# Which items of a mixture-of-experts plan are followed by transposes, scatters and slot numbers

## The chip, the cores and the metric

The kernel runs on one core of one Trainium2 chip. The metric is the device time of one execution in microseconds (us). Every instruction of TensorE (PE), VectorE (DVE), ScalarE (ACT), GpSimd (POOL) and the DMA queues is in the profile of one such execution.

## The reference

One layer of a decoder: RMSNorm, a pooling mixer beside latent attention, an output projection, and then a mixture of 32 experts, of which each of the 512 tokens takes 4. The change lies in the mixture of experts alone. Cut to that part:

```python
logits = (ht @ w_router + b_router).astype(jnp.float32)
top_vals, top_idx = lax.top_k(logits, TOP_K)
gates = jax.nn.softmax(top_vals, axis=-1)
...
def expert_block(args):
    xblk, e = args
    gu = xblk @ w_gate_up[e] + b_gate_up[e]
    gate = jnp.minimum(gu[:, :D_EXPERT], SWIGLU_LIMIT)
    up = jnp.clip(gu[:, D_EXPERT:], -SWIGLU_LIMIT, SWIGLU_LIMIT)
    act = gate * jax.nn.sigmoid(SWIGLU_ALPHA * gate) * (up + 1)
    return act @ w_down[e] + b_down[e]
...
y = y.at[row_tok].add(row_gate[:, None] * yb)
```

The model dimension and the experts' dimension are 1024, everything is float32, and the weights of the 32 experts are 384 MiB, which are read once.

## The kernel before

The first 200 us or so of the span compute the layer up to the router (phase A); the rest is the mixture of experts. The 32 experts stand in 32 **positions**, which are named by their number here. `KINDS` makes 12 of them big (2, 4, 6, ... 24) and 20 small. A big position takes up to 128 tokens. Its float32 weights are split into a high part (`mhi`, cast by ACT, L937) and a low part (`mlo`, a subtraction on DVE, of every fourth half on POOL, L938), and every product is three matmuls: high by high, high by low, low by high. A small position takes up to 64 tokens, and its product uses the float32 weights as they are, in 64 columns of the array; two matmuls run side by side on the two halves of the columns.

A position is 12 **items**: gate/up items 0 to 7 and down items 0 to 3, each with one load of 1 MiB. So there are 384 items. A big item is 12 matmuls of 128 columns (the generators `gate_up` and `down` yield once in its middle), a small one 4 matmul instructions, which the trace shows as 8 records (a yield never comes in it). `interleave` puts the items of two lanes into one order, the list `plan`: the lane x (`onx`) holds the big positions and positions 0 and 31, the lane y the other small ones. Loads are issued 14 items ahead, on SP's queue, into a ring.

Beside the items stands work that is small but has to come at some time. It sits in five **queues** of Python generators, and `step()` lets each queue go on by one step:

- `turn x` and `turn y`: `turn(r)` transposes the activation of a position (`m<-ident,au`, four transposes to a step; two steps for a big position, one for a small one). It is queued after the last gate/up item, and `later(..., 3)` spends three steps first. The result is copied out of PSUM by ACT (`ath`, or `ats` at L1036 for a small position) and, for a big one, by DVE also (`atl`). The down items need it: `step(("turn x",))` or `step(("turn y",))` before a down item 0 runs the queue dry.
- `gather`: `gather(r)` transposes the fetched rows of a position (`m<-ident,xr`, two steps of four transposes). For a big position each of the 8 transposes is split in a **chunk** of its own, ACT's `xgh` (L894) and then DVE's `xgl` (L895), both of which read the PSUM bank; a small pair's is one DVE operation for a step (`xgs`). The first gate/up item of the position needs it.
- `arrive`: slot numbers (`m<-aux,oh`) of a position, and then the indirect DMA that fetches its rows (L881, POOL).
- `rest`: the scatters (`combine`): eight steps, each a pair of matmuls `m<-ybh,sc` and `m<-ybl,sc` (for a big position) or `m<-ysh,ss` and `m<-ysl,ss` (for two small ones) and one addition on DVE into `y` (L1148).

All of this work goes through the PSUM pool `m`, which has **two banks** that are taken in turn; the pools `x` (4 banks) and `y` (2) hold the items' products. A matmul into a bank of `m` waits until the one who used that bank two steps ago has been read out. PE runs strictly in the order in which the program is written, from item 12 on (`InOrder`, L118 is the helper's line for every PE instruction). So where `step()` stands, there the transposes and scatters stand on PE. Before the change `step()` is called at the yield in the middle of a big item and at the end of every item of both lanes:

```python
for _ in gate_up(r, k) if what == "gu" else down(r, k):
    step()
...
step()
```

`turn_at` and `fetch_at` say behind which item a gather and a fetch are queued. At a down item 3, `while ("b" if big(r) else "s") in pending: step()` runs the scatters of the position before dry, since their buffers are written anew there.

Of the kernel before, what the change touches and what calls it, by code (L numbers as in the profile page):

```python
# [51 lines left out]
GAPX, GAPY, GAPN, GAPEND = 5, 2, 1, 3  # L52
TURN, SHORT = 0.2, 3.0
NFREE = 12
FILL1 = 2
FT = 3
FN = ((0, 1), (1, 3), (1, 3), (3, 4))
# [68 lines left out]
def block_kernel(ctx: ExitStack, tc: tile.TileContext, xT, x, pos, vecs, w_in, w_pool, w_qb, w_kvb, w_out,  # L126
# [277 lines left out]
    for g, w in enumerate(WINDOWS):  # L404
        cur, step, lo_ = us[g], 1, 1
# [138 lines left out]
    def out_proj(z, c, tt):  # L544

        cs = slice(c * T, (c + 1) * T)
        for k in range(4):
            if ("out", z, c, k) in wraw:
                parts[z, c, k] = split_w(("out", z, c, k))
        po = {}  # L550
        for k in range(4):
            for t in tt:
                if k == 0:
                    po[t] = pt("po", bufs=5 if c and z else 7)
                ts = slice(t * P, (t + 1) * P)
                mm3(PE, po[t], mix["h", z][:, k, ts], mix["l", z][:, k, ts], *parts[z, c, k], k == 0, k == 3)
                yield
        for t in tt:
            V.scalar_tensor_tensor(y[:, t, cs], po[t], grms[z][:, t:t + 1], y[:, t, cs], op0=ALU.mult, op1=ALU.add)
# [193 lines left out]
    for t in range(NT):  # L753
        for _ in out_proj(1, 1, [t]):
            for _ in range(FILL1):
                while todo and next(todo[0], 0) == 0:
# [26 lines left out]
    def bank(tag):  # L783
        return pools["pm"].tile([P, T], F32, tag=tag, bufs={"x": 4, "y": 2, "m": 2}[tag], name=tag)
# [57 lines left out]
    onehot, slots, xg, yb, scat, actT = {}, {}, {}, {}, {}, {}  # L842

    def big(r):
        return r == "o" or KINDS[r] == "B"

    def onx(r):

        return big(r) or r == 0 or r == E - 1
# [103 lines left out]
    def fixed(r):  # L953
        return r != "o" and r < NFIX

    def biases(r, cs):
        for c in cs:
            bs = bias[:, c * T:(c + 1) * T]
            if big(r):
                PE.matmul(banks[r][c], lhsT=m4b[0:96, r:r + 1].to_broadcast([96, P]), rhs=bs, start=True, stop=False)  # L960
            else:
                q = 64 * (c % 2)
                PE.matmul(banks[r][c // 2][q:q + 64, :], lhsT=m4b[0:96, r:r + 1].to_broadcast([96, 64]), rhs=bs,
                          start=not fixed(r), stop=fixed(r))

    def gate_up(r, k):

        first = r == "o"
        if k == 0:
            banks[r] = [bank("x" if onx(r) else "y") for _ in range(4 if big(r) else 2)]  # L970
        if big(r):

            todo = [(hf, c) for hf in range(2) for c in range(2)] if k < KD - 1 else [
                (hf, c) for c in range(2) for hf in range(2)]
            parts = presplit.pop((r, "gu", k))
            for n, (hf, c) in enumerate(todo):
                cs = slice(c * T, (c + 1) * T)
                if k == 0 and not first:
                    biases(r, [2 * hf + c])
                mm3(PE, banks[r][2 * hf + c], xg[r][0][:, k, :], xg[r][1][:, k, :], parts[hf][0][:, cs],  # L980
                    parts[hf][1][:, cs], first and k == 0, k == KD - 1)
                if n == 1:
                    yield
        else:
            w = wslots.pop((r, "gu", k))
            for c in range(4):
                q = 64 * (c % 2)
                if k == 0 and c % 2 == 0 and not fixed(r):
                    biases(r, [c, c + 1])
                PE.matmul(banks[r][c // 2][q:q + 64, :], lhsT=xg[r][:, k, :], rhs=w[:, c * T:(c + 1) * T],  # L990
                          start=(k == 0 and fixed(r)), stop=(k == KD - 1 and not fixed(r)))

                if k == KD - 1 and c % 2 == 1 and fixed(r):
                    biases(r, [c - 1, c])
# [444 lines left out]
    groups = {}  # L1439
# [6 lines left out]
    def arrive(r):  # L1446

        for q in groups[r]:
            select(q)
            yield  # L1450
            slot_info(q)
        fetch(r)
# [28 lines left out]
    def firsts(g):  # L1481
        return plan.index(("gu", g, 0))
# [4 lines left out]
    bigs = [r for r in range(E) if big(r)]  # L1487
# [6 lines left out]
            assert fetch_at[g] > KD, g  # L1494
    queues = {"turn x": [], "turn y": [], "gather": [], "arrive": [], "rest": []}

    def step(drain=None):

        for name, q in queues.items():
            if drain and name not in drain:  # L1500
                continue
            while q:
                if next(q[0], 0) == 0:
                    q.pop(0)
                elif not drain:
                    break
# [21 lines left out]
    for i, (what, r, k) in enumerate(plan):  # L1528

        PE.on = i >= NFREE  # L1530
        while loaded < min(i + (14 if i > 2 else 9), len(loads)):
            load(*loads[loaded])
            loaded += 1
        if big(r):
            n = xorder.index((what, r, k))
            assert n < nsp
        for g, at in fetch_at.items():
            if at == i:
                queues["arrive"].append(arrive(g))
        for g, at in turn_at.items():  # L1540
            if at == i:
                queues["gather"].append(gather(g))
        if (what, r, k) == ("gu", E - 1, 0):
            gf = mo.tile([P, D], F32, tag="xgh", bufs=1, name="gf")
            dma(gf[0:1, :], g_final)
        if k == 0 and what == "gu" and r > 0:
            assert r in xg, (r, i)
        if what == "dn" and k == 0:
            step(("turn x" if onx(r) else "turn y",))
        if what == "dn" and k == KD // 2 - 1:  # L1550

            while ("b" if big(r) else "s") in pending:
                step()
        if (what, r, k) == ("dn", E - 1, 0):
            step(queues)
            down_last(r, gf)
            break
        for _ in gate_up(r, k) if what == "gu" else down(r, k):
            step()

        ahead = n + 3 if big(r) else 2 if (what, r, k) == ("dn", 0, KD // 2 - 2) else 0
        for v in xorder[nsp:ahead]:
            split_item(v[1], v[0], v[2])
        nsp = max(nsp, min(ahead, len(xorder)))
        if what == "gu" and k == KD - 1:
            if r == E - 1:
                spread(gf)
            queues["turn x" if onx(r) else "turn y"].append(later(turn(r, act(r)), 3))
        if what == "dn" and k == KD // 2 - 1 and r < E - 2:
            if big(r):  # L1570
                queues["rest"].append(later(marked("b", combine([r])), 3))
            elif halfdone[0] is None:
                queues["rest"].append(later(marked("s", combine(["s"], r < NFIX)), 3))
        step()
    rt.close()

    PE.on = False
# [95 lines left out]
```

## Time and profile before

| what | value |
|---|---|
| median of three runs | 1267.49 us (1266.92 to 1268.07) |
| the profiled execution, its own time | 1268.17 us |
| its span in the trace | 1266.4 us |
| PE busy | 1213.0 us, 96% of the span |
| DVE, ACT, POOL busy | 865.4, 542.7, 303.7 us |
| DMA: bytes, mean rate | 435.17 MB, 344 GB/s |

The span is the time between the first and the last instruction in the trace; 1.8 us of the execution lie around it. A timeline row of PE gives the start, the duration, the line, the tiles and the count of equal instructions that follow each other. Since the matmuls overlap at their ends, what a group costs is best read as the difference of two starts. A bracket at a row's end is the idle time of the engine before it, and who released it.

### The profile page before, as it was taken

The page shows a single profiled execution, that of the slowest core. Times are in us where ns is not written, and L with a number is a line of the kernel's source. Part 1 is how long each engine was busy: PE and PEld are TensorE (multiplying, and loading weights), DVE is VectorE, ACT ScalarE, POOL GpSimd, SP SyncE. Part 2 cuts the span into 40 slices and gives each one's busy share as a digit, 9 for nine tenths or more (in the row PEclk, how much of TensorE's full clock was granted, in tenths as well). Part 3 has the DMA queues.
Part 4 walks back from the last instruction along what each step waited for, and adds up shares of the span by engine and source line. Part 5 has one row for each costly group of instructions (what it writes and reads, how often), then busy time and mean ns, then how long its engine had stood idle before and what let it go on. Part 6 is the DMA issues. An engine that isn't in the chain of part 4 may idle for free.

```text
span 1266.4 us, 16525 instructions
## 1 busy us (share of the span) xinstructions
PE 1213.0 (96%) x5597; PEld 697.3 (55%) x5597; DVE 865.4 (68%) x1552; ACT 542.7 (43%) x785; POOL 303.7 (24%) x272
## 2 busy tenths in 40 slices
PE   7979999899999998999999999999999999999994
PEld 6856674345655555555555555555645555555332
DVE  6897674657767676676768667776765876767344
ACT  6466650135525443354354435435434454444013
POOL 2355362112212121221123113221312122212001
PEclk9999999899999998999999999999999999999997
DMA  8312428999999998999998999999999999999981
GB/s 313 100 51 88 146 90 313 409 421 415 416 419 411 404 405 322 360 413 416 402 377 348 420 388 399 402 386 393 381 416 358 361 421 403 377 380 399 422 333 69
DMA packets 86849, 435.17 MB, mean 344 GB/s; under 512 B 9223, under 2 KB 9223, under 8 KB 53992
## 3 DMA queue, kind: packets, MB, share of 16 engines
q1 hardware_dynamic: 82818, 420.43, 83.4%
q0 software_dynamic: 3744, 13.24, 2.7%
q8 instruction: 45, 0.74, 0.2%
q10 hardware_dynamic: 198, 0.39, 0.1%
q14 instruction: 44, 0.36, 0.1%
HBM read 429.71 MB, written 4.33 MB: 343 GB/s over the span
## 4 chain that ended last, share of the span: by engine, by line
PE 74%; DVE 7%; DMA 1%; issue 1%; ACT 1%; POOL 0%; DVEq 0%; ACTq 0%; POOLq 0%
PE x L118 33%; PE y L118 29%; PE m L118 11%; DVE mlo L938 3%; DMA bdraw<-in_b_down_dram 1%; DVE au L1007 1%; ACT mhi L937 1%; DVE oh L859 0%; DVE au L1008 0%; DVE ag L1004 0%; DVE au L1006 0%; DVE xgl L895 0%; DVE ss L1096 0%; DVE y L1130 0%; DVE o L1186 0%
## 5 line engine op out<-in xcount | busy, mean ns | idle before, releaser
L937 ACT CAST mhi<-slot 128x1024 fp32r<-128x1024 f32 x288 | 300.6, 1049 | 260.9 <-PE x L118 236.1
L938 DVE TENSOR_TENSOR mlo<-slot,mhi 128x1024 fp32r<-128x1024 f32 x216 | 288.3, 1347 | 66.3 <-ACT mhi L937 65.8
L938 POOL TENSOR_TENSOR mlo<-slot,mhi 128x1024 fp32r<-128x1024 f32 x72 | 177.4, 2464 | 642.5 <-ACT mhi L937 642.4
L118 PE MATMUL y<-slot,xgs 128*64 128x512 f32 x1152 | 276.0, 602 | 0.0
L1148 DVE TENSOR_TENSOR y<-y,m 128x512 f32<-128x512 f32 x168 | 115.0, 684 | 121.8 <-PE m L118 121.4
L118 PE MATMUL x<-mhi,xgh 128*128 128x512 f32 x384 | 164.0, 427 | 0.0
L118 PE MATMUL x<-mlo,xgh 128*128 128x512 f32 x384 | 152.0, 396 | 0.1
L118 PE MATMUL x<-mhi,xgl 128*128 128x512 f32 x384 | 151.4, 394 | 0.0
L118 PEld LDWEIGHTS y<-slot,xgs 128*64 128x64 f32 x1152 | 76.1, 137 | 130.4 <-issue 126.9
L118 PE MATMUL y<-slot,ats 128*64 128x512 f32 x608 | 144.5, 612 | 0.7 <-ACT ats L1036 0.7
L1005 ACT ACTIVATE as<-ag 128x512 f32<-128x512 f32 x44 | 27.8, 632 | 160.7 <-DVE ag L1004 160.7
L118 PEld LDWEIGHTS x<-mhi,xgh 128*128 128x128 f32 x384 | 72.7, 189 | 25.7 <-issue 12.2
L118 PEld LDWEIGHTS x<-mhi,xgl 128*128 128x128 f32 x384 | 72.1, 188 | 17.0
L118 PEld LDWEIGHTS x<-mlo,xgh 128*128 128x128 f32 x384 | 72.4, 189 | 15.9 <-DVE mlo L938 1.1
L118 PEld LDWEIGHTS y<-slot,ats 128*64 128x64 f32 x608 | 39.7, 138 | 74.3 <-issue 70.5
L118 PE MATMUL x<-mhi,ath 128*128 128x512 f32 x192 | 64.2, 416 | 0.0
L118 PE MATMUL x<-mlo,ath 128*128 128x512 f32 x192 | 61.4, 401 | 0.0
L118 PE MATMUL x<-mhi,atl 128*128 128x512 f32 x192 | 60.9, 398 | 0.0
L1098 ACT ACTIVATE ysh<-y,sl 64x512 fp32r<-64x512 f32 x36 | 24.6, 684 | 80.4 <-PE y L118 80.1
L1100 DVE SCALAR_TENSOR_TENSOR ysl<-y,sl,ysh 64x512 fp32r<-64x512 f32 x36 | 27.0, 750 | 42.4 <-ACT ysh L1098 41.9
L881 POOL DMA_INDIRECT xr<-hrow,idx x21 | 28.7, 1367 | 94.5 <-DVE idx L878 48.7
L894 ACT ACTIVATE xgh<-m,gs 128x128 fp32r<-128x128 f32 x96 | 33.4, 366 | 31.9 <-PE m L118 16.7
(401 smaller groups left out, 1737.1 us busy)
## 6 DMA issues: line engine op xcount, KB each, us to landing
slot<-in_w_gate_up_dram SPq DMA_DIRECT2D x256, 1024.0 KB, 10.4
slot<-in_w_down_dram SPq DMA_DIRECT2D x128, 1024.0 KB, 9.9
wraw<-in_w_in_dram SPq DMA_DIRECT2D x16, 256.0 KB, 5.7
wraw<-in_w_out_dram SPq DMA_DIRECT2D x16, 256.0 KB, 2.6
xtraw<-in_xT_dram SPq DMA_DIRECT2D x8, 256.0 KB, 5.9
y<-in_x_dram SPq DMA_DIRECT2D x4, 512.0 KB, 7.3
hrow<-part POOLq DMA_DIRECT2D x8, 256.0 KB, 3.3
out_dram<-o SPq DMA_DIRECT2D x4, 512.0 KB, 2.7
```

Of the source, the lines that this page charges most:

```text
L118: r = f(*args, **kwargs)
L881: G.indirect_dma_start(out=rows[r], out_offset=None, in_=hrow, in_offset=bass.IndirectOffsetOnAxis(ap=idx[:, 0:1], axis=0), bounds_check=T ...
L894: S.activation(hi[:, d, :], v, AF.Copy, scale=g)
L937: S.copy(hi, src)
L938: eng.tensor_tensor(lo, src, hi.bitcast(F32), op=ALU.subtract)
L1005: S.activation(sg, g, AF.Sigmoid, scale=1.702)
L1007: V.scalar_tensor_tensor(u, u, 1.0, g, op0=ALU.add, op1=ALU.mult)
L1098: S.activation(yh[ps_, c], db[ps_, :], AF.Copy, scale=slots[r][ps_, 6:7])
L1100: V.scalar_tensor_tensor(yl[ps_, c], db[ps_, :], slots[r][ps_, 6:7], yh[ps_, c].bitcast(F32), op0=ALU.mult, op1=ALU.subtract)
L1148: V.tensor_tensor(y[:, t, cs], y[:, t, cs], pb, op=ALU.add)
```

## The change

`step` gets a second argument, `only`, with the names of the queues that may go on. Behind the items of the lane y (from the first item of the first big position on) `only` is `("turn x",)`, and `("turn x", "gather")` where the first gate/up item of a big position lies at most `SOON` = 4 items ahead and its gather hasn't been done. So of a small position's item nothing follows but big positions' transposes; scatters, slot numbers, fetches and the transposes of small positions' activations and rows stand behind items of the lane x, in their middle or at their end. A gather that isn't done at its position's first item is run there.

```diff
+SOON = 4
...
-    def step(drain=None):
+    def step(drain=None, only=None):
 
         for name, q in queues.items():
-            if drain and name not in drain:
+            if name not in (drain or only or queues):
                 continue
...
         if k == 0 and what == "gu" and r > 0:
-            assert r in xg, (r, i)
+            while r not in xg:
+                step(only=("gather",))
...
+        beside = None if onx(r) or i < firsts(bigs[0]) else ("turn x",)
+        if beside and any(0 < firsts(g) - i <= SOON and g not in xg for g in groups if big(g)):
+            beside += ("gather",)
         for _ in gate_up(r, k) if what == "gu" else down(r, k):
-            step()
+            step(only=beside)
...
-        step()
+        step(only=beside)
```

The plan of items, the loads and the ring are the same. PE's lines are L118 before and L119 after. Three places on PE show what moves.

**Place 1: gate/up items 4 to 7 of small position 11, between gate/up items 2 and 3 of big position 8.** The matmuls `y<-slot,xgs` are the small items, four to an item, `x<-...` the big ones, and `m<-ybh,sc` and `m<-ybl,sc` a scatter pair. Before:

```order
L118 MATMUL m<-ybh,sc 128x512
L118 MATMUL m<-ybl,sc 128x512
L118 MATMUL y<-slot,xgs 64x512 x4
L118 MATMUL m<-ybh,sc 128x512
L118 MATMUL m<-ybl,sc 128x512
L118 MATMUL y<-slot,xgs 64x512 x4
L118 MATMUL m<-ybh,sc 128x512
L118 MATMUL m<-ybl,sc 128x512
L118 MATMUL y<-slot,xgs 64x512 x4
L118 MATMUL m<-ybh,sc 128x512
L118 MATMUL m<-ybl,sc 128x512
L118 MATMUL y<-slot,xgs 64x512 x4
```

After:

```order
L119 MATMUL y<-slot,xgs 64x512 x16
L119 MATMUL x<-mhi,xgh 128x512
L119 MATMUL x<-mlo,xgh 128x512
L119 MATMUL x<-mhi,xgl 128x512
L119 MATMUL x<-mhi,xgh 128x512
L119 MATMUL x<-mlo,xgh 128x512
L119 MATMUL x<-mhi,xgl 128x512
L119 MATMUL m<-ybh,sc 128x512
L119 MATMUL m<-ybl,sc 128x512
```

The four small items stand together, and the scatter pairs that stood behind each of them come later, in the middles and at the ends of big items.

**Place 2: the gather of big position 4, in the down items of position 2.** `m<-ident,xr` are the gather's two blocks of transposes, `m<-aux,oh` slot numbers. Before:

```order
L118 MATMUL m<-ident,xr 128x128 x4
L118 MATMUL x<-mhi,ath 128x512 x2
L118 MATMUL x<-mlo,ath 128x512 x2
L118 MATMUL x<-mhi,atl 128x512 x2
L118 MATMUL m<-ident,xr 128x128 x4
L118 MATMUL x<-mhi,ath 128x512 x2
L118 MATMUL x<-mlo,ath 128x512 x2
L118 MATMUL x<-mhi,atl 128x512 x2
```

After:

```order
L119 MATMUL m<-ident,xr 128x128 x4
L119 MATMUL x<-mhi,ath 128x512 x2
L119 MATMUL x<-mlo,ath 128x512 x2
L119 MATMUL x<-mhi,atl 128x512 x2
L119 MATMUL m<-ident,xr 128x128 x4
L119 LDWEIGHTS oh
L119 MATMUL m<-aux,oh 128x4
```

The slot numbers, which use the bank of the first block, now stand right behind the second block; before, items of positions 2 and 3 stood there.

**Place 3: the transposes of small position 15, ahead of its down items.** `m<-ident,au` are the transposes, `y<-slot,ats` the down items that use them, and `x<-...` halves of a down item of position 10. Before:

```order
L118 MATMUL m<-ident,au 128x128 x4
L118 MATMUL x<-mhi,ath 128x512 x2
L118 MATMUL x<-mlo,ath 128x512 x2
L118 MATMUL x<-mhi,atl 128x512 x2
L118 MATMUL y<-slot,ats 64x512 x12
```

After:

```order
L119 MATMUL x<-mhi,ath 128x512 x2
L119 MATMUL x<-mlo,ath 128x512 x2
L119 MATMUL x<-mhi,atl 128x512 x2
L119 MATMUL m<-ident,au 128x128 x4
L119 MATMUL y<-slot,ats 64x512 x16
```

The half of a big item that stood between the transposes and the down items is gone from there.

## Rows read from the trace of the kernel before

**Rows 1.** The page: busy time, share, count; one line of the costliest groups.

```profile
PE 1213.0 (96%) x5597; PEld 697.3 (55%) x5597; DVE 865.4 (68%) x1552; ACT 542.7 (43%) x785; POOL 303.7 (24%) x272
...
L938 DVE TENSOR_TENSOR mlo<-slot,mhi 128x1024 fp32r<-128x1024 f32 x216 | 288.3, 1347 | 66.3 <-ACT mhi L937 65.8
L1148 DVE TENSOR_TENSOR y<-y,m 128x512 f32<-128x512 f32 x168 | 115.0, 684 | 121.8 <-PE m L118 121.4
```

**Rows 2.** Windows: us; busy PE, PEld, DVE, ACT, POOL; PEclk, DMA share, GB/s.

```profile
250.00:400.00 150.00, 150.00 (x686) 81.88 (x683) 103.86 (x158) 65.17 (x84) 29.77 (x14) 1.00 1.02 416
400.00:700.00 300.00, 291.55 (x1318) 167.79 (x1316) 214.25 (x323) 134.06 (x171) 69.19 (x31) 0.98 0.96 385
```

**Rows 3.** Timeline of PE: a scatter pair between halves of a big item.

```profile
508.06 0.40 PE L118 MATMUL m<-ybh,sc 128*128 128x512 f32 x1
...
508.53 0.40 PE L118 MATMUL x<-mhi,xgh 128*128 128x512 f32 x1
```

**Rows 4.** Timeline of PE: two small items; a small item and a scatter pair.

```profile
295.73 3.65 PE L118 MATMUL y<-slot,ats 128*64 128x512 f32 x16
299.32 0.25 PE L118 MATMUL m<-aux,oh 128*128 128x4 f16 x4
...
514.20 1.94 PE L118 MATMUL y<-slot,xgs 128*64 128x512 f32 x8
516.07 0.50 PE L118 MATMUL m<-ybh,sc 128*128 128x512 f32 x1
...
516.74 1.94 PE L118 MATMUL y<-slot,xgs 128*64 128x512 f32 x8
```

**Rows 5.** Timeline of PE: blocks of transposes among small items, and in a big one.

```profile
392.40 0.66 PE L118 MATMUL m<-ident,au 128*128 128x128 f32 x4
...
394.85 0.66 PE L118 MATMUL m<-ident,au 128*128 128x128 f32 x4
...
761.81 0.60 PE L118 MATMUL m<-ident,au 128*128 128x128 f32 x4
762.16 0.48 PE L118 MATMUL x<-mhi,xgh 128*128 128x512 f32 x1
```

**Rows 6.** Timeline of PE at the gather of position 8: blocks, next scatter.

```profile
475.56 0.60 PE L118 MATMUL m<-ident,xr 128*128 128x128 f32 x4
...
477.85 0.60 PE L118 MATMUL m<-ident,xr 128*128 128x128 f32 x4
...
482.69 0.79 PE L118 MATMUL m<-ysh,ss 128*128 128x512 f32 x1 [4.24 <-DVE xgl L895]
```

**Rows 7.** Waits of the whole span: us in total, times, longest.

```profile
PE m L118 <- DVE xgl L895: 9.2, 4, 4.2
```

**Rows 8.** Timeline of PE, ACT and DVE at the gather of position 22.

```profile
1019.64 0.66 PE L118 MATMUL m<-ident,xr 128*128 128x128 f32 x4
...
1020.34 0.37 ACT L894 ACTIVATE xgh<-m,gs 128x128 fp32r<-128x128 f32 x1 [1.82 <-PE m L118]
1021.12 0.37 ACT L894 ACTIVATE xgh<-m,gs 128x128 fp32r<-128x128 f32 x1 [0.42 <-DVE xgl L895]
...
1023.19 0.61 DVE L895 SCALAR_TENSOR_TENSOR xgl<-m,gs,xgh 128x128 fp32r<-128x128 f32 x2 [0.53 <-ACT xgh L894]
...
1028.16 0.25 PE L118 MATMUL m<-aux,oh 128*128 128x4 f16 x4
```

**Rows 9.** Windows behind two waits, columns as in the second group.

```profile
482.60:486.00 3.40, 3.31 (x8) 2.64 (x9) 1.07 (x3) 0.18 (x1) 0.00 (x0) 0.50 1.02 424
486.00:490.00 4.00, 4.00 (x14) 3.14 (x13) 2.00 (x3) 1.63 (x2) 0.00 (x0) 0.69 0.66 270
...
645.00:649.00 4.00, 4.00 (x14) 2.16 (x14) 3.08 (x5) 3.71 (x7) 2.04 (x1) 0.57 0.59 211
```

**Rows 10.** Timeline of ACT and PE: a small position's transposes, their copy, their use.

```profile
763.01 0.58 ACT L1036 COPY ats<-m 128x512 f32<-128x512 f32 x1
...
763.73 1.94 PE L118 MATMUL y<-slot,ats 128*64 128x512 f32 x8
```

## The prediction, made before the changed kernel ran

> **What bounds the kernel now.** I read the busy times first, then the windows, then PE's timeline around the transposes and scatters, then the waits. PE is busy for 96% of the span, no other engine for more than 68% [rows 1]. By stage: from 250 to 400 us PE is busy for all of the 150 us, from 400 to 700 for 291.55 of 300 [rows 2]. So the experts' part is bound by PE, and whatever PE's own order costs or saves counts in full. The DMA share stands at 0.96 to 1.02 there [rows 2], so the weights' stream is nearly a bound too; I come back to that as a rival. The time of PE consists of the items themselves, which the change leaves alone, the price of what stands between them, and some waits. The waits that matter are those for a bank of `m` whose last chunk of a gather isn't split yet: 9.2 us in four waits, the longest 4.2 [rows 7].
>
> All sums below are made against the profiled execution, 1268.2 us; the median of the three runs is 0.7 lower.
>
> **A. What is taken out: returns to small items.** PE uses its array whole for big items, scatters and transposes, and in two column halves for small items, and each change between the two shows in the starts. A pair of scatters between halves of a big item takes 508.06 to 508.53, 0.47 us [rows 3]. A small item with a pair behind it takes 514.20 to 516.74, 2.54 us, while two small items in a row take 295.73 to 299.32, 3.59 us, of which 0.09 is the change at the end, as in the next step, so 1.75 for one [rows 4]. So the same pair costs 0.79 behind a small item that is followed by another: 0.32 more. A block of transposes among small items costs 392.40 to 394.85, 2.45, less 1.75, so 0.70; in a big one 0.35 for the block and 0.09 for the first matmul behind it (0.48 instead of 0.39), 0.44 [rows 5]: 0.26 more. Counted in the two orders from the first big position to item 356, work stands between two small items 80 times before and 28 times after. Of the 52 that go, 38 have scatters and 14 have transposes or slot numbers alone (I take the transposes' price for all of these): 38 x 0.32 + 14 x 0.26 = **-15.8 us**. This is the surest term.
>
> The Trainium skill ("TensorEngine Tiling (Array Packing)", Key Properties) says that a change of the tiling mode drains TensorE; it gives no time for it. The trace agrees in kind, with the 0.32 above.
>
> **B. What takes its place: waits behind big gathers.** Place 2 shows it. The scatters, slot numbers and small transposes that used to be spread over items of both lanes now come at every step in the big lane, and a gather is queued in the same lane. So the third user of `m`, which gets the bank of the gather's first block, comes much sooner after it. When is that bank free? Its four chunks each need ACT and then DVE, and DVE has low parts of weights, 1.35 us each, in its queue among them [rows 1]. Only three big gathers before the change had somebody waiting at their first bank: at position 8 the first block starts at 475.56, the next scatter gets through at 482.69 after a wait of 4.24, 7.13 us later [rows 6]; the other two (positions 12 and 20) lie within 0.2 us of that, with waits of 2.0 and 2.7. These three make 8.9 of the 9.2 us [rows 7]. At the other gathers the next user came 8 to 17 us after the first block and nobody waited, as at position 22: 1019.64 to 1028.16 [rows 8].
>
> In the new order the third user comes, if nothing holds it up, 2.3 us after the first block at positions 4, 8 and 10, 2.75 at 24, about 5.1 to 5.6 at 12, 14, 18 and 22; at 6 and 20 a first wait stands ahead of the second block. (The times are counts of halves of big items, 1.4 us each, and of the blocks, from the rows above.) With the bank free at 7.1 us, the waits are 4.8 at 4, 8 and 10, 4.3 at 24, 3.6 at 6, 2.7 at 20, 1.5 at 12 and 18, 2.0 at 14 and 22: 32.0, less the 8.9 of before, **+23.1 us**. The low end: the bank is free when its fourth chunk is out at the earliest that the trace shows, 1023.19 + 0.35 against 1019.64, 3.9 us [rows 8]; then 6.4 us of waits are left, -2.5 net. The high end: at 12, 14, 18 and 22 the new order of DVE has two evictions of a big position and a low part ahead of the first block's last chunk, about 3 us of work, so that the bank is free at about 10; +35. I take 7.1, the value of the only gathers at which somebody waits, as here.
>
> Why a chunk takes so long is in the rows too: even with both engines free the chunks follow each other 0.78 us apart (1020.34, 1021.12), ACT and DVE by turns [rows 8]. The Trainium skill ("PSUM — Partial Sum Buffer", PSUM bank collisions raise a hardware error) says that two engines must not touch one bank in the same partitions at once, readers included, which speaks against bringing bank users together. The alternation in the rows is what that rule would give; by it no bank is free before 4 x 0.78 = 3.1 us, which doesn't change the sum.
>
> **C. The clock behind such waits.** Behind the wait of 4.24 us the granted clock reads 0.50 from 482.6 to 486 and 0.69 to 490; behind that of position 12, 0.57 from 645 to 649 [rows 9]. (1 - 0.50) x 3.4 + (1 - 0.69) x 4 = 2.9 us lost, and (1 - 0.57) x 4 = 1.7; position 20 reads as 1.7 in the same way, so 6.3 for three waits of 2 us or more, 2.1 each. With eight such waits 16.8, less 6.3: **+10.5** (from -3, if one or two waits are left, to +21).
>
> **D. Transposes of small positions.** They stand directly ahead of their down items in several places (place 3), where half a big item used to lie between. The copy by ACT ends 1.78 us after the start of the transposes at 761.81, and with six big matmuls between, the down items at 763.73 had 0.14 us to spare [rows 5, 10]. Without them PE waits 1.3 us (0.9 to 1.7, as ACT is free or casting a high part); with a scatter pair between, 0.65. Position 9: 1.3; positions 5, 19, 21, 28 and 17, with something between: 5 x 0.65. Positions 15, 23 and 25 are behind gathers and counted there. **+4.6** (2.5 to 6).
>
> **E. A flush.** At position 27's last down item five scatter pairs and two blocks of transposes now stand in a row, since fewer steps were left for them. A pair takes PE 0.47 and DVE's addition 0.68 [rows 1, 3], so at least 5 x 0.21 = 1 us, up to 6 where low parts stand in DVE's queue; **+3.5**.
>
> **F. The last 45 us.** Eight returns fewer (-2.6), ten scatter pairs in a row at position 30 (+3), about 1 to 2 us of today's waits gone: **-1** (-3 to +3).
>
> Indirect fetches are queued later as well; the rows they bring are used a few items later, and place 2 shows the gathers themselves at the same place. I put that at nothing; if the cover is gone, it shows as one more wait of some 2 us. The loads of weights are issued at the same items as before.
>
> **The sum:** -15.8 + 23.1 + 10.5 + 4.6 + 3.5 - 1 = +24.9, so 1293.1 for a profiled execution, 1292 for the median.
>
> **The rivals.**
>
> *The banks come free early.* PE that waits leaves ACT and DVE less to do, and the chunks get through as at position 22, 3.9 us after the block. Then B is -2.5, C is -3 and D to F about +2.5: 1268.2 - 15.8 - 2.5 - 3 + 2.5, **1249**. The point from which it decides is a bank free at about 5.3 us: there B is +5, C about +3 and the whole comes to no change. Against it: the three gathers with a waiting user, all at 7. For it: 7 us is three of twelve, and their order on DVE need not be that of the others.
>
> *The weights' stream becomes the bound.* With PE faster by 18 us, the DMA share of 0.96 to 1.02 leaves perhaps 10 us: **1258**. It only cuts the gain of the first rival.
>
> *The work comes behind small items all the same.* The flushes and `turn x` steps could leave most of the returns in place, and the waits too: about **1266**. The order speaks against it: 28 of 80 are left.
>
> *The long waits.* If the four gathers with evictions ahead of their chunks free their bank at 10 us, B is +35 and C +19: **1313**.
>
> **How the numbers follow.** Forecast, waits at 6 to 9 us: 0.56, between 1276 and 1306. A weaker form with some banks free at 5.5 to 6 us, 1270 to 1276: 0.12. No change, with early and late ones in balance or the work where it was: 0.08. Early banks, with or without the stream as the bound: 0.19. Long waits, over 1308: 0.05. The predicted time is the forecast's. For 8 in 10 the range takes in much of the early case: 1254 to 1308; the forecast's own range is 1276 to 1306. About 0.2% is what a measurement of this kernel can tell from no change. Faster 0.19, same 0.08, slower 0.73.
>
> **What would show it.** A: the starts of small items in a row, 1.75 to 1.8 us apart, and 52 groups fewer between them; PE's time between small items at 0.79 and 0.70 as before where it's left. B: the wait of PE in `m` for `xgl`, 9.2 us before, at about 30 in some ten waits, each ending about 7 us after a gather's first block; if it stays under 12, B is wrong. C: stretches at a granted clock of 0.5 to 0.7 behind those waits. D: waits for `ats` of about 1 us ahead of down items of the small positions. E: a row of scatter pairs at position 27 with waits for `y`. The prediction is wrong if banks come free under 5.3 us after the block, or if PE's waits are in other places than behind the gathers, the new order of the fetches above all.

## The result, and the profile after

The changed kernel takes 1311.46 us (median of four runs, 1310.69 to 1311.87), against 1267.78 for the kernel before in the same comparison: a ratio of 1.0346 (95% interval 1.0332 to 1.036), 43.7 us slower. The prediction was slower, 1292, in a range up to 1308. The direction was right and most of the places were; the size was not.

The page of the kernel after, busy times, and two windows (columns as in rows 2):

```profile
span 1310.1 us, 16514 instructions
...
PE 1214.0 (93%) x5597; PEld 710.9 (54%) x5597; DVE 864.7 (66%) x1552; ACT 543.8 (42%) x785; POOL 311.2 (24%) x272
```

```profile
400.00:700.00 300.00, 279.55 (x1259) 165.89 (x1258) 202.11 (x309) 127.53 (x162) 64.41 (x28) 0.97 0.92 366
700.00:1000.00 300.00, 276.94 (x1243) 157.80 (x1243) 202.90 (x299) 127.59 (x164) 65.74 (x30) 0.97 0.93 365
```

PE is busy for the same time as before [rows 1], 1214 us, and the span is 43.7 us longer. So all of the loss shows as idle PE: 20.4 of 300 us from 400 to 700, 8.4 before [rows 2]. The DMA share has fallen from 0.96 to 0.92, and none of PE's waits from the first big item on is for a load of weights, so the weights' stream isn't what holds PE. The waits of the whole span (us in total, times, longest), as in rows 7:

```profile
PE m L119 <- DVE xgl L896: 36.4, 10, 6.6
...
PE y L119 <- ACT ats L1037: 6.7, 8, 1.6
...
PE m L119 <- DVE y L1149: 3.9, 7, 1.5
...
PE m L119 <- ACT ats L1037: 1.8, 3, 1.2
```

The first of them was 9.2 in four [rows 7]. That PE's busy time is unchanged hides two things of opposite sign: fewer returns to small items, and matmuls that take about twice as long at half clock (a scatter's matmul 0.80 us at 744.82 below, 0.40 in rows 3). To part them I took PE's timeline of each run from the first matmul of a big item to the last matmul, and split it in three: the gaps between records; at half clock, half of the busy time there; and the rest, which holds the work at full clock and so the returns. The part ahead of the first big item has the same code in all kernels but took 269 to 276 us in the profiled executions, which isn't explained here; the table leaves it out. (Half clock means stretches whose granted clock is 0.50.)

| kernel | time, us | part with big items | waits for a big gather | waits for `ats` | other idle | half clock | rest |
|---|---|---|---|---|---|---|---|
| before | 1267.8 | 981.0 | 9.2 | 0.7 | 3.5 | 8.0 | 959.6 |
| after | 1311.5 | 1023.7 | 36.4 | 8.6 | 12.3 | 19.5 | 946.9 |
| scatters_only | 1275.8 | 987.9 | 21.2 | 1.1 | 5.8 | 11.5 | 948.3 |
| all_but_scatters | 1319.9 | 1030.9 | 28.7 | 13.9 | 9.2 | 19.2 | 959.9 |
| hold_after | 1294.8 | 1006.7 | 19.7 | 7.8 | 14.1 | 16.4 | 948.6 |
| turn_y_after | 1300.2 | 1010.2 | 35.1 | 1.6 | 10.3 | 17.6 | 945.6 |
| fast_before | 1256.5 | 971.4 | 0 | 2.7 | 4.0 | 4.8 | 959.9 |
| fast_after | 1267.1 | 978.3 | 3.0 | 12.6 | 11.5 | 3.1 | 948.0 |
| four_ops_after | 1268.4 | 980.8 | 4.7 | 11.5 | 11.8 | 4.8 | 948.1 |
| fast_turn_y | 1250.6 | 961.5 | 1.9 | 1.6 | 10.9 | 0 | 946.9 |
| fast_scatters | 1249.2 | 963.3 | 2.4 | 1.1 | 6.7 | 4.8 | 948.2 |
| fast_turns_gathers | 1258.6 | 971.7 | 4.2 | 1.6 | 10.7 | 4.8 | 950.4 |

(The times are medians, the other columns come from one profiled execution each. Most lie within 3 us of the median; that of fast_before took 1263.4, that of all_but_scatters 1324.5.) From before to after: rest -12.7, gather waits +27.2, `ats` +7.9, other idle +8.8, half clock +11.5, and 1.0 ahead of the first big item: +43.7.

### The profile page after: what moved, and what is told of

It reads as the page before. It is cut to its first block, busy times and chain, and to the rows that moved or that the text cites. A ratio compares the mean times of both kernels' runs of the same rounds, so it can differ in the third digit from the quotient of the medians.

```text
span 1310.1 us, 16514 instructions
## 1 busy us (share of the span) xinstructions
PE 1214.0 (93%) x5597; PEld 710.9 (54%) x5597; DVE 864.7 (66%) x1552; ACT 543.8 (42%) x785; POOL 311.2 (24%) x272
## 4 chain that ended last, share of the span: by engine, by line
PE 82%; DVE 11%; ACT 3%; issue 2%; DMA 0%; SPq 0%; DVEq 0%; ACTq 0%
PE x L119 32%; PE y L119 30%; PE m L119 9%; PE po L119 3%; PE acc L119 3%; DVE mlo L939 3%; ACT mhi L938 2%; PE s L119 1%; PE pa L119 1%; DVE xgl L896 1%; DVE y L1149 1%; PE pp L119 1%; PE rows L119 1%; DVE oh L860 0%; ACT ats L1037 0%
## 5 line engine op out<-in xcount | busy, mean ns | idle before, releaser
L939 POOL TENSOR_TENSOR mlo<-slot,mhi 128x1024 fp32r<-128x1024 f32 x72 | 183.0, 2541 | 700.8 <-ACT mhi L938 700.7
L119 PE MATMUL y<-slot,xgs 128*64 128x512 f32 x1152 | 273.6, 609 | 0.0
L119 PE MATMUL x<-mhi,xgh 128*128 128x512 f32 x384 | 164.6, 429 | 0.0
L119 PEld LDWEIGHTS y<-slot,xgs 128*64 128x64 f32 x1152 | 80.4, 139 | 143.1 <-issue 140.5
L119 PE MATMUL x<-mlo,xgh 128*128 128x512 f32 x384 | 151.9, 396 | 1.5 <-DVE mlo L939 1.3
L119 PE MATMUL x<-mhi,xgl 128*128 128x512 f32 x384 | 151.2, 394 | 0.0
L119 PE MATMUL y<-slot,ats 128*64 128x512 f32 x608 | 141.2, 613 | 6.7 <-ACT ats L1037 6.7
L119 PEld LDWEIGHTS x<-mhi,xgh 128*128 128x128 f32 x384 | 72.7, 189 | 34.5 <-issue 21.1
L119 PEld LDWEIGHTS y<-slot,ats 128*64 128x64 f32 x608 | 42.1, 140 | 89.6 <-issue 79.7
L119 PEld LDWEIGHTS x<-mlo,xgh 128*128 128x128 f32 x384 | 72.4, 188 | 17.2 <-DVE mlo L939 2.8
L119 PEld LDWEIGHTS x<-mhi,xgl 128*128 128x128 f32 x384 | 72.1, 188 | 17.2
L119 PE MATMUL x<-mhi,ath 128*128 128x512 f32 x192 | 66.3, 428 | 0.0
L119 PE MATMUL x<-mlo,ath 128*128 128x512 f32 x192 | 62.0, 405 | 0.0
L119 PE MATMUL x<-mhi,atl 128*128 128x512 f32 x192 | 61.5, 403 | 0.0
L119 PEld LDWEIGHTS x<-mhi,ath 128*128 128x128 f32 x192 | 34.3, 196 | 19.0 <-issue 13.8
```

The costliest lines, as they stand in the source:

```text
L119: r = f(*args, **kwargs)
L939: eng.tensor_tensor(lo, src, hi.bitcast(F32), op=ALU.subtract)
```

## The mechanism in one gather

PE's timeline of the kernel after at the gather of position 14, where the trace of before shows no wait:

```profile
734.58 0.60 PE L119 MATMUL m<-ident,xr 128*128 128x128 f32 x4
...
736.42 0.60 PE L119 MATMUL m<-ident,xr 128*128 128x128 f32 x4
...
739.16 0.62 PE L119 MATMUL x<-mhi,atl 128*128 128x512 f32 x2
744.82 0.80 PE L119 MATMUL m<-ysh,ss 128*128 128x512 f32 x1 [5.04 <-DVE xgl L896]
```

and DVE's and ACT's timelines in the same stretch:

```profile
736.15 1.23 DVE L939 TENSOR_TENSOR mlo<-slot,mhi 128x1024 fp32r<-128x1024 f32 x1
737.41 0.35 DVE L896 SCALAR_TENSOR_TENSOR xgl<-m,gs,xgh 128x128 fp32r<-128x128 f32 x1
738.02 0.61 DVE L896 SCALAR_TENSOR_TENSOR xgl<-m,gs,xgh 128x128 fp32r<-128x128 f32 x2 [0.26 <-ACT xgh L895]
739.56 1.72 DVE L939 TENSOR_TENSOR mlo<-slot,mhi 128x1024 fp32r<-128x1024 f32 x1 [0.93 <-ACT mhi L938]
741.20 0.59 DVE L896 SCALAR_TENSOR_TENSOR xgl<-m,gs,xgh 128x128 fp32r<-128x128 f32 x2
741.72 1.39 DVE L1067 SCALAR_TENSOR_TENSOR ybl<-x,sl,ybh 128x512 fp32r<-128x512 f32 x2
743.04 1.21 DVE L939 TENSOR_TENSOR mlo<-slot,mhi 128x1024 fp32r<-128x1024 f32 x1
744.17 0.59 DVE L896 SCALAR_TENSOR_TENSOR xgl<-m,gs,xgh 128x128 fp32r<-128x128 f32 x2
```

```profile
738.48 1.05 ACT L938 CAST mhi<-slot 128x1024 fp32r<-128x1024 f32 x1 [0.23 <-ACT xgh L895]
739.44 0.61 ACT L895 ACTIVATE xgh<-m,gs 128x128 fp32r<-128x128 f32 x2
739.95 1.26 ACT L1066 ACTIVATE ybh<-x,sl 128x512 fp32r<-128x512 f32 x2
```

The scatter that follows gets through at 744.8, when the seventh chunk (the second of the pair at 744.17) is out. It is the seventh and not the fourth because the program's order on DVE alternates between the two banks: in the built program, whose tile numbers the trace leaves out, the chunks of this gather read `m_6256`, `m_6283`, `m_6256`, `m_6283` and so on. The first bank holds out until its fourth chunk, which is the seventh of the eight. Two low parts of weights and two evictions of position 12 lie among them, in DVE's order, which doesn't know that PE waits. Over the whole kernel, the user that waits gets through at the seventh chunk at positions 8, 10, 12, 14, 16, 18 and 22, at the fourth at 4, 6 and 24, where the order on DVE has the first bank's four in a row (at 6 it is the gather's own second block that waits). In the program of the kernel before, of these gathers only 4 and 8 alternate in this way: with PE's order the change has altered DVE's order too. The pool doesn't hand out its banks strictly in turn, as I put it ahead of the prediction. At position 12 a scatter stands between the blocks:

```profile
649.44 0.60 PE L119 MATMUL m<-ident,xr 128*128 128x128 f32 x4
649.79 0.48 PE L119 MATMUL m<-ysh,ss 128*128 128x512 f32 x1
...
652.03 0.66 PE L119 MATMUL m<-ident,xr 128*128 128x128 f32 x4
...
662.10 1.11 PE L119 MATMUL m<-ident,au 128*128 128x128 f32 x4 [6.62 <-DVE xgl L896]
```

The second block starts 2.6 us after the first with hardly a wait, in the scatter's bank, since the first block's is in use for 10 us more.

## The experiments

All edits are to the changed kernel unless the label says before. The order of PE was changed only where the edit says so.

**One operation empties the bank.** fast_after and fast_before:

```diff
             if big(r):
-                for i in range(4):
-                    split_rows(4 * b + i, v[:, i, :])
+                hs, ls = hi[:, 4 * b:4 * b + 4, :], lo[:, 4 * b:4 * b + 4, :]
+                xv = mo.tile([P, 4, P], F32, tag="ag", bufs=1, name="xv")
+                V.tensor_tensor(xv, v, gs[:, 4 * b:4 * b + 4].unsqueeze(2).to_broadcast([P, 4, P]), op=ALU.mult)
+                S.copy(hs, xv)
+                V.tensor_tensor(ls, xv, hs.bitcast(F32), op=ALU.subtract)
```

> The changed kernel, but a big gather's bank is emptied by one DVE operation of four chunks into SBUF (0.7 us), from which ACT and DVE then make the high and low parts; nothing else moves. Theory (the chain of eight ACT-DVE chunks holds the bank, and both the waits and the half clock come from it): PE's waits for the gather's evictions fall from 36 us to under 8, stretches at half clock from 51 us to under 15, time 1311.5 - 29 - 18 = about 1264 (1255 to 1275). Rival (the bank is late because DVE works through low parts of weights first, however few operations the eviction has): waits of 20 us are left, half clock 30 us, time about 1288.

Measured: 1267.1 us, 0.9991 of before (0.9977 to 1.0004), 44 us under the changed kernel with this edit alone. The gather of position 14 now, on PE and DVE:

```profile
712.28 0.60 PE L119 MATMUL m<-ident,xr 128*128 128x128 f32 x4
...
714.10 0.60 PE L119 MATMUL m<-ident,xr 128*128 128x128 f32 x4
...
717.31 0.39 PE L119 MATMUL m<-ysh,ss 128*128 128x512 f32 x1
```

```profile
712.32 1.51 DVE L1104 SCALAR_TENSOR_TENSOR ysl<-y,sl,ysh 64x512 fp32r<-64x512 f32 x2 [5.27 <-ACT ysh L1102]
713.87 0.69 DVE L917 TENSOR_TENSOR xv<-m,gs 128x512 f32<-128x512 f32 x1
714.48 1.22 DVE L942 TENSOR_TENSOR mlo<-slot,mhi 128x1024 fp32r<-128x1024 f32 x1
```

The bank is free at 714.6, 2.3 us after the first block, though `ysl` stood ahead of it on DVE until 713.8. (A low part that stood between `ysl` and the first chunk in the kernel after now stands behind the operation, so DVE's order has moved a little too.) Over the twelve gathers the first bank is free 1.3 to 4.8 us after its block; at the ten that wait in the kernel after it was 4.7 to 12.7. The scatter at 717.31 waits for nothing. Waits for gathers fall from 36.4 to 3.0, the loss at half clock from 19.5 to 3.1. The theory holds, the rival (DVE's queue as such) doesn't. The time is 3 us over the theory's 1264; beside that, the waits for `ats` grew from 8.6 to 12.6.

> The kernel before with the same one-operation eviction of a big gather's bank. Theory: its 9 us of waits go and the 14 us at half clock with them (about 7 lost), so 1267.8 - 9 - 7 = about 1252, with the returns to small items as they were. Rival (DVE's queue is what holds the bank): under 4 us faster, about 1265.

Measured: 1256.5, ratio 0.9904 (0.9886 to 0.9922). The waits are gone to the last; the time is 4 us above the expectation; the waits for `ats` have grown by 2.0. So the quick eviction gives 11 us without the change, and of the change's own loss of 44 it takes away 33. Between the two kernels with the quick eviction the change still loses 10.6 us in the medians, 6.9 of them in the part with big items: its returns give 11.9 (959.9 to 948.0) and the clock 1.7, while `ats` takes 9.9, other idle 7.5 and the gathers 3.0.

**Is it the number of operations?** four_ops_after, the same with four DVE operations to a bank in the place of one:

```diff
-                V.tensor_tensor(xv, v, gs[:, 4 * b:4 * b + 4].unsqueeze(2).to_broadcast([P, 4, P]), op=ALU.mult)
+                for i in range(4):
+                    V.tensor_scalar(xv[:, i, :], v[:, i, :], gs[:, 4 * b + i:4 * b + i + 1], None, op0=ALU.mult)
```

> As fast_after, but a big gather's bank is emptied by four DVE operations, one for each chunk, and then split from SBUF. So the number of DVE operations on the bank is that of the changed kernel, and only their alternation with ACT's is gone; in DVE's order the four stand in a row. Theory (what holds the bank is that each chunk goes to ACT and back to DVE, with other work of DVE between the chunks): bank free about 2 us after the block, waits under 8, time 1265 to 1274. Rival (four small operations behind DVE's queue are as slow as the chunks were): waits over 20, time over 1285.

Measured: 1268.4, waits for gathers 4.7. On DVE at position 14:

```profile
717.82 1.13 DVE L918 TENSOR_SCALAR xv<-m,gs 128x128 f32<-128x128 f32 x4
718.87 1.22 DVE L943 TENSOR_TENSOR mlo<-slot,mhi 128x1024 fp32r<-128x1024 f32 x1
```

Four operations in a row take 1.13 us. So it isn't their number that held the bank for 5 to 13 us. What is left is that every chunk went to ACT and back, that the two banks took turns, and that DVE's order had other work between; the edit removes the three together, and no run parts them.

**The work right behind a gather is held back.** hold_after:

```diff
+            if hold[0] and not drain and name in ("turn y", "arrive", "rest"):
+                continue
...
+        hold[0] = max(0, hold[0] - 1)
...
+            if big(r):
+                hold[0] = HOLD
             yield
```

> The changed kernel, but behind each block of a big gather the scatters, slot numbers and small turns are held back for six steps (turns that a down item forces, and flushes, are not); the eviction is the old one with eight chunks. The third user of the two banks then comes 5 to 20 us after the first block instead of 2 to 5. Theory: waits for the evictions fall from 36 us to about 10, half clock from 51 to about 15, a few us come back as scatters in a row: 1311.5 - 26 - 18 + 5 = about 1272. Rival (work that is held only moves its wait to the next place, since steps in the big lane are too few): over 1295.

Measured: 1294.8, ratio 1.0209 (1.0191 to 1.0227): better than the change by 17 us, and not what I expected. 19.7 us of waits are left in six. At 4, 8, 14, 22 and 24 they are gone; at 6, 12, 18 and 20 it is the small positions' transposes, which a down item forces out whatever the hold says, and at 10 and 16 a scatter that a flush forces. The rival is right in part: where a deadline stands behind the held work, the wait only changes its place.

**The parts of the change by themselves.** scatters_only and all_but_scatters:

```diff
-        beside = None if onx(r) or i < firsts(bigs[0]) else ("turn x",)
+        beside = None if onx(r) or i < firsts(bigs[0]) else ("turn x", "turn y", "gather", "arrive")
```

```diff
-        beside = None if onx(r) or i < firsts(bigs[0]) else ("turn x",)
+        beside = None if onx(r) or i < firsts(bigs[0]) else ("turn x", "rest")
```

> One part of the change alone: only the scatters are kept from behind small items; turns, gathers and slot numbers stand behind items of both lanes as before. 38 returns with scatters fewer (-12 us). By the order the third user of the banks comes within 2.6 us of the first block at positions 6, 8 and 24, at 2.1 at 12 and about 5.6 at 18. Theory (the price of a wait is 7 us less that time, and half clock behind it): waits about 23 us, half clock 30 us: 1267.8 - 12 + 14 + 8 + 3 = about 1281. Rival (the move of slot numbers and gathers made the waits): waits as before, 1267.8 - 12 + 3 = about 1259.

Measured: 1275.8, ratio 1.0056 (1.0037 to 1.0076). Its waits:

```profile
PE m L119 <- DVE xgl L896: 21.2, 7, 4.7
```

21.2 us against the 23 that came from the order. The waits at 6, 8, 12 and 24 are there as named (4.1, 4.7, 4.4 and 2.5), the one at 18 is not, and 16 and 20, which it didn't name, have 2.6 and 2.7: the sum is in part luck. The gain of the returns is 11.3 in the rest.

> The other part of the change alone: turns of small positions, gathers and slot numbers are kept from behind small items as in the changed kernel, the scatters stay behind items of both lanes. By the order the third user comes 2.1 us after the first block at positions 4 and 10, at 0.4 to 2.6 at 6, 8 and 20, at 3.5 to 4.9 at 12, 14, 18 and 22. Theory (waits come from what stands right behind a gather, whichever kind of work it is): waits for the evictions 33 us, waits for ats 8, 15 returns fewer (-4): 1267.8 - 4 + 24 + 10 + 8 = about 1306. Rival (it is the scatters that clump): under 1280.

Measured: 1319.9, ratio 1.0403 (1.0382 to 1.0425), worse than the whole change and 14 us above the expectation: the returns' 4 us did not come, `ats` took 6 more than its 8, and other idle and the part ahead of the first big item grew by some 6 each against before, while the gathers' waits are 4 under the forecast (all in the profiled execution). Its waits:

```profile
PE m L119 <- DVE xgl L896: 28.7, 8, 5.3
...
PE y L119 <- ACT ats L1037: 8.4, 9, 1.6
...
PE m L119 <- ACT ats L1037: 5.5, 2, 4.2
```

So the scatters aren't what is needed for the waits: slot numbers and small transposes do as well (at six of the eight; at two it is a scatter that waits). And the rest is 959.9, as before the change: the 15 returns that this part removes saved nothing that the split can show. Nearly all of the gain, 11.3 of 12.7, comes from the scatters.

**The turns of small positions.** turn_y_after, and fast_turn_y with the quick eviction:

```diff
-        beside = None if onx(r) or i < firsts(bigs[0]) else ("turn x",)
+        beside = None if onx(r) or i < firsts(bigs[0]) else ("turn x", "turn y")
```

> The changed kernel, but the turns of small positions may stand behind small items too, as before the change; scatters, slot numbers and gathers as in the changed kernel. Theory (7.7 us of waits for ats come from turns that stand right ahead of their down items): those fall under 2 us, the waits for evictions stay at 33 to 38: about 1305. Rival (the copy to ats is late because of the waits at the gathers, not the place of the turn): ats still over 6, time 1310.

Measured: 1300.2, ratio 1.0253 (1.0236 to 1.027), 11 us under the change: `ats` falls from 8.6 to 1.6, the gathers' waits stay at 35.1, the half clock costs 2 less.

> turn_y_after with the one-operation eviction. In fast_after 11.7 us of waits for ats are left, the largest wait there. Theory: they fall under 2 us, so 1267.1 - 10 = about 1257. Rival: as above, 1265.

Measured: 1250.6, ratio 0.9862 (0.9845 to 0.9878), 16.5 us under fast_after and better than expected. `ats` gives 11.0 of it, the half clock 3.1.

**Which mixture is best.** fast_scatters is scatters_only with the quick eviction; fast_turns_gathers has `("turn x", "turn y", "gather")` and the quick eviction.

> Both: only the scatters are kept from behind small items, and a big gather's bank is emptied by one operation. Theory (the scatters' move is a gain of about 11 us whose waits all hang on the gathers' banks): from scatters_only the 21 us of waits go and 8 of half clock: main part 911 - 27 = 884, time 1275.8 - 27 = about 1248, under the kernel before with the quick eviction (1256.5) by 8. Rival (the gain of fewer returns is smaller than the rows say, or is lost to scatters in a row): no better than 1256.

Measured: 1249.2, ratio 0.9844 (0.9822 to 0.9865). The theory's number. It beats both kernels, the one before by 18.7 us and the changed one by 62; from fast_turn_y's 1250.6 its four runs (1245.7 to 1251.4) can't be told. Its windows:

```profile
400.00:700.00 300.00, 294.26 (x1357) 173.77 (x1357) 223.53 (x320) 133.79 (x151) 71.35 (x32) 0.99 0.99 397
700.00:1000.00 300.00, 297.23 (x1352) 170.56 (x1349) 217.44 (x307) 129.58 (x147) 68.54 (x29) 1.00 1.00 404
```

From 700 to 1000 PE is busy for 297 of 300 us and the DMA share is 1.00 at once. Which of the two holds it there isn't shown.

> The changed kernel with the one-operation eviction, and with the turns of small positions and all gathers behind items of both lanes; only scatters and slot numbers are kept from behind small items. Between two small items 42 returns are left, against 28 in fast_turn_y and 47 in fast_scatters. Theory: rest of the main part as fast_turn_y + 14 x 0.2 = 877, waits as in fast_scatters (8), so about 1250, with neither of the two. Rival (slot numbers behind small items cost more than the rows say): 1246.

Measured: 1258.6, ratio 0.9926 (0.991 to 0.9943): 8 us above the expectation, and the rival is wrong too. Against fast_turn_y it has 10.2 us more in the part with big items: 3.5 in the rest, as expected, 2.1 of waits, 4.8 at half clock. The waits differ at one place: a scatter behind the gather of position 12 waits 2.39, since the one operation ends only 4.8 us after the block there (fast_scatters has the same wait), and a stretch at half clock behind it costs 1.7. The other 3.1 at half clock are a stretch at 1208.8 with no wait of 1 us ahead of it, which fast_turn_y's execution doesn't have.

## Why the prediction was wrong

Term by term, forecast and measured (us):

| term | forecast | measured |
|---|---|---|
| A, with the returns of F | -18.4 | -12.7 |
| B, waits behind big gathers | +23.1 | +27.2 |
| C, half clock, tail included | +10.5 | +11.5 |
| D, `ats` | +4.6 | +7.9 |
| E and the waits of F | +5.1 | +8.8 |
| ahead of the first big item | 0 | +1.0 |
| sum | +24.9 | +43.7 |

(F's -1 is split here into its returns, -2.6, its scatters in a row, +3, and the waits of before that I let go, -1.4, of which the trace shows nothing; a late stretch at half clock in before, 1.7, is gone and stands in C.) Every term has the right sign, and every error the same one, 18.8 us in all. The large causes are the forecast ones. The step that failed is the sizing of four terms: A, 5.7 too much gain; B, one release of 7.1 us for every gather where 4.7 to 12.7 were measured, 4.1 too little; D, 3.3 too little, 2.6 of it at three positions counted as covered that were not; and E and F, 3.7 too little, since some 7 us are waits that no term had. The range was built around the middle values of these terms.

**A was too large** by 5.7. The price of a pair of scatters behind a small item was nearly right, 0.28 us for 0.32: scatters_only has 33 returns fewer, and 8 in the last part, and gains 11.3, and small items in a row do follow each other at the expected 1.75:

```profile
503.47 6.17 PE L119 MATMUL y<-slot,xgs 128*64 128x512 f32 x28
509.57 0.39 PE L119 MATMUL x<-bias,m4b 96*128 96x512 bf16 x1
```

(6.10 us for 3.5 items, in PE's timeline of the kernel after.) But the 14 moved transposes and slot numbers were priced by a row too, 0.26 each, and all_but_scatters shows nothing for them. I took a difference of two single rows as the price of a move. The rows of the old place don't say what the new place costs; why nothing was saved, no run shows.

**B was right in sum and wrong in its parts.** The sum was 32.0, measured 36.4 in ten waits, as forecast. I gave all gathers one release, 7.1 us. In the program of before, the chunk that emptied the first bank was the seventh at 8, the fourth at 12 and the sixth at 20, so nothing in the order made all three about 7 us. At 4, 8, 10, 24 and 6 I forecast 4.8, 4.8, 4.8, 4.3 and 3.6 and the waits were 2.2, 4.2, 3.2, 1.2 and 1.2; at 12, 14, 18 and 22 I forecast 1.5, 2.0, 1.5 and 2.0 and they were 6.6, 5.0, 5.1 and 5.0; one of 2.6 at 16 I did not have, and the 2.7 at 20 did not come. Those four are the gathers for which the prediction itself says that DVE's order has evictions and a low part ahead of the last chunk, with the bank free at about 10. It is what came (the users got through 10.2 to 12.7 us after the first block), and I put it into the high end and left it out of the value. The bound of 3.9 us, and with it the first rival, rested on the fourth chunk in time; where the banks alternate it is the seventh that counts. (At position 22 before it was the fifth, which ends at 1023.80, 4.2 us after the block.)

**C was right** within 1 us in sum, with some luck. I had eight waits of 2 us or more at 2.1 each, 16.8, and eight there were; with a ninth stretch behind two shorter waits at position 6 they cost 19.5, one more, another less. What brings the difference down to 11.5 is the late stretch of before, 1.7, which stands behind no wait of 1 us and which I had not counted. The windows behind the waits at positions 14 (the first row) and 18 (the two others):

```profile
744.80:749.00 4.20, 4.18 (x12) 1.62 (x14) 1.04 (x2) 0.11 (x1) 0.00 (x0) 0.50 1.02 423
...
912.20:916.00 3.80, 3.13 (x10) 1.44 (x12) 0.35 (x1) 0.63 (x2) 0.00 (x0) 0.50 0.94 319
916.00:920.00 4.00, 4.00 (x12) 0.95 (x8) 0.00 (x0) 0.00 (x0) 0.00 (x0) 0.52 0.38 117
```

At 14 that is half of 4.18, 2.1 us, for a wait of 5.0; at 18 half of 3.13 + 0.48 x 4.0, 3.5 us, for a wait of 5.1.

**D was too small**, 4.6 against 7.9. Positions 15, 23 and 25 I had counted as covered by the waits at the gathers. At 15 and 23 PE waited 0.7 each for `ats` behind those, and the second block of position 20's gather waited 1.2 for such a copy: 2.6 of the 3.3. The price, too, was taken from one row where ACT had one high part to cast; at position 9 it had two, and PE waited 1.63 where I had 1.3. PE's and ACT's timelines of the kernel after:

```profile
469.62 0.60 PE L119 MATMUL m<-ident,au 128*128 128x128 f32 x4
471.85 2.37 PE L119 MATMUL y<-slot,ats 128*64 128x512 f32 x10 [1.63 <-ACT ats L1037]
```

```profile
469.21 1.98 ACT L938 CAST mhi<-slot 128x1024 fp32r<-128x1024 f32 x2
471.21 0.58 ACT L1037 COPY ats<-m 128x512 f32<-128x512 f32 x1
```

**E and F cost little, and waits at other places took their room.** The rows of scatter pairs came, but cost little: the five pairs and two blocks, from 1043.0 on, have 0.9 us of gaps (0.7 of it for `atl`) where I had 3.5, the ten pairs at position 30 have 0.8 besides `ats` where I had 3. The other 7 us of the 8.8 are waits that no term had: for `y` at three other places (1.5, 0.6 and 1.0, which with position 30 make the 3.9), for a small pair's gather (`xgs`, 1.5 at one place, 0.4 before), for low parts (1.3), and for index arithmetic on DVE (1.2) and fetched rows (0.3), which I had put at nothing. That they come from the work standing closer together is argued, not shown.

**The rivals.** The banks didn't come free early. With quick banks the change takes 1267.1 (fast_after) and not the rival's 1249, since `ats` (12.6) and the other idle (11.5) cost far more than its +2.5; fast_turn_y comes to 1250.6, but with the turns moved as well. The stream was not the bound (share 0.92 and 0.93), as long as PE waited; with the waits gone it reads 0.99 and 1.00 and may be one. The work was not behind small items all the same. The rival of the long waits, 1313, had a chance of 0.05 and its mechanism is the one that decided at four gathers. That its 1313 lies near the measured time is luck: it has B at 35 and C at 19 where 27.2 and 11.5 came, too large a gain in A, and too little for D, E and F.

On the Trainium skill's two rules ("TensorEngine Tiling (Array Packing)", Key Properties; "PSUM — Partial Sum Buffer", PSUM bank collisions raise a hardware error): the first agrees with the 0.28 us that a return with scatters costs here. The second is compatible with ACT and DVE by turns on one bank, but no run here has them on one bank at once, and the alternation at its quickest, four chunks at 0.78 us, is 3.1 of the 4.7 to 12.7 us for which the bank was held.

## What to carry to other kernels

Before work is moved next to other work, look at the buffer that both use and ask when it comes free: not how long its eviction takes in the profile at a place where nobody waits, but what stands between its parts in the evicting engine's queue, in the order of the changed program. An eviction that goes through two engines in pieces is a good one to shorten first: copy the bank out in one operation, and split from SBUF; here that took 33 us off the change's loss of 44 and gave 11 us without the change, and the scatters' part of the change with it is 19 us faster than the kernel before. And when several terms are each taken at a middle value, an error that they share (here, every price came from the trace of before, where this work stood farther apart) adds up on one side, so the range has to be wider on that side than any one term makes it.

## What the runs showed of the hardware

A wait of PE of about 2 us or more was nearly always followed by a stretch with a granted clock of 0.50, at 1.2 GHz. From the first big item on the twelve profiled executions have 48 such waits, and 43 were, all eight in the kernel after among them; those of 2.70 and 2.45 us at positions 20 and 24 in scatters_only, of 2.62 in turn_y_after, of 2.46 in fast_after and of 2.11 in four_ops_after were not. Nor is there always a wait in front: eight of the executions have a stretch at 0.50 late in the span, between 1199 us and the last matmul, with no wait of 1 us in the 8 us ahead of it. In the twelve kernels the loss at half clock runs beside the waits for gathers, from 0 to 5 us where those are under 5, to 11 to 20 where they are 19 to 37 (8.0 beside 9.2 in the kernel before). So in the kernel after the waits at the gathers cost about half of their length again (19.5 beside 36.4), which the idle time in a profile doesn't show, since matmuls at half clock count as busy.
